# A hybrid attention block on one core: first rows turned by a product with a diagonal, rotary in 1024 columns, queries' sums in the unit stream

## The chip, the core and the metric

The kernel runs on one core of one Trainium2 chip. The core has a matrix engine (TensorE, PE in the profile, with its weight loads shown apart as PEld), three engines that work on 128 partitions (VectorE or DVE, ScalarE or ACT, GpSimd or POOL), a queue engine (SyncE or SP), and DMA queues, which SP, ACT and POOL start. PE writes its products into PSUM, eight banks of 512 fp32 columns. The metric is the device time of one execution in microseconds (us).

## The reference

One decoder layer on x (1024 tokens, 1024 channels), in fp32:

```python
h = rmsnorm(x, norm_w)                       # x * rsqrt(mean(x*x) + eps) * norm_w
proj = h @ w_in                              # 9232 columns
q_a, k_a = rope(q, cos, sin), rope(k, cos, sin)
o_a = dilated_mixture(q_a, k_a, v_a)         # three groups: dilation 1, 4, 16; 8 heads of 64
y_a = (o_a * silu(dsa_z)) @ w_up_a
cqkv = silu(causal_conv(gdn_qkv, conv_w))    # gated delta rule, 8 heads, chunks of 64
gq, gk = l2norm(gq) * 64**-0.5, l2norm(gk)
o_b = rmsnorm(gated_delta_rule(gq, gk, gv, g, beta), gdn_norm_w)
y_b = (o_b * silu(gdn_z)) @ w_up_b
out = rmsnorm(x + (sigmoid(gate_a)*y_a + sigmoid(gate_b)*y_b) @ w_out, final_norm_w)
```

rope takes each head's two halves a, b of 32 channels to a cos - b sin and b cos + a sin. The delta rule needs, per chunk and head, the inverse of a unit lower triangular 64 by 64 matrix.

## The kernel before

**Numbers in two halves.** Every fp32 matrix that enters a large product is split into fp16 high and low parts, and a product is three matmuls (high by high, high by low, low by high). The normalised input, transposed, is kept as h_hi and h_lo (channels on partitions, tokens along the columns) for the whole kernel. ACT makes the high part (a copy to fp16), DVE the low part (a scalar_tensor_tensor, STT, L82, or tensor_tensor, TT, L85; all such operations have the helper's line).

**The start (L390 to L560).** Tokens 0 to 511 come as rows (xt, four blocks of 128 tokens), tokens 512 to 1023 already transposed. For a block of rows, `rstd_rows` (L442) has ACT square and sum, and DVE invert the root; `scale_rows` multiplies the rows by that factor and by the norm weights (nwr, 512 KB, the weights repeated on all partitions); `turn_rows` (L457) has PE transpose eight squares of 128 into two PSUM banks ("G"); `split_rows` (L462) evicts each bank of 512 columns, ACT the high and DVE the low part. Meanwhile `rows_product` (L470) makes the first query and key units, a block of rows at a time. PE's, ACT's and DVE's order is written out by hand there.

**The unit stream.** All other projections are units of 256 weight columns, kept in a list by the class `Feed`. `feed.tick(n)` emits n steps of the current unit; a step, a tick, is three matmuls (12 small ones in V units). A unit has 32 ticks, or 28 where a seven-product scheme (`seven_products`) saves an eighth. `feed.later(n, fn)` emits fn n ticks later, `feed.until(name)` runs to a unit's end, `feed.flush()` until nothing is left for later. PE's order is this program order throughout; the other engines and the queues follow a planner's order, in which `tc.high_priority` moves work ahead.

**Rotary.** A query or key unit gives two channel tiles (a and b) for two halves of 512 tokens. `rope_evict` (L583) copies each from PSUM into a tile rx of 512 columns (three buffers); `rope_half` (L592) makes, when a and b of a half are there, four products with the tables (tabs, 1 MB, cosines and sines), a difference and a sum (ro), and writes each as high (ACT, L607) and low (DVE) parts into pc tiles, in an order by residue modulo the dilation DIL[g] (1, 4, 8 for groups 0, 1, 2), which it reads with a stride. `rope_out` (L611) spreads them by DMAs on SP into Qh, Ql and Ks.

**Attention (`att_run`, L711).** Six sets (group, half of the heads), groups 2, 1, 0, each in 16 steps: scores (PE L767, L769 into bank "S"), masked minimum (DVE L776), exp (ACT L780), transposes (PE L790 into "G"), split (ACT L795, DVE L85 tl), values (PE L813 to L817 into "O"). Between its parts the next set's units run by ticks. For group 0, `combine` (L840) merges the three groups on DVE; its two transposes (PE L876) come TURN_LAG ticks later.

**The linear attention.** After the last set, `decay` makes E by PE, `keys_side` (L1219) sums the keys' squares by `sumsq` (L1189: for two of eight token blocks, four transposes into bank "S", L1196, ACT squares in place, L1201, DVE sums, L1202, then two ticks) and multiplies key pairs (`pairs`, L1205), `solve` (L1253) loads them through DRAM as As, does the triangular solve X of 32 by 32 blocks on DVE, and writes X and its transpose to DRAM (L1275, L1276); they come back as MT and T1p (L1284, L1282, issued on SP). `merge` (L1287) joins the 32 blocks to 64 on PE (L1299, L1314), inside `state_side`. Heads go in two halves, hb 0 and 1. For the queries (L1593 on): after unit ("gdn", hb, 0), Q_LAG[hb] ticks, `pairs`, `spill`, `sumsq`, and for hb 0 STATE_LAG ticks and `state_side(1)`. The sums rq are first used in the scan over chunks that follows gate unit 5. After the scan come output gates, the up projection, the output product and the final norm.

The functions that the change touches:

## Time and profile before

| what | value |
|---|---|
| median of 3 runs | 1096.39 us (1093.91 to 1096.77) |
| the profiled execution, its own time | 1097.13 us |
| its span, first to last instruction | 1095.4 us |
| mean granted TensorE clock | 0.995 |
| busy ACT, POOL | 572.1 us (52%), 65.4 us (6%) |
| DMA moved | 146.89 MB, 134 GB/s |

In a timeline row stand the start and duration in us, engine, line, operation, output and inputs, shapes, and in brackets how long the engine was idle before it and what ended that. In a row of groups stand the count, the busy time in us, the mean of one in ns, and the idle time ahead. In a wait row stand the total, the number and the longest. In a row of stretches stand the length and, for PE, PEld, DVE, ACT and POOL, busy us and instructions, then the granted clock (1 is full), the DMA share and GB/s. Matmuls are pipelined, so PE's durations overlap, and the spacing of starts is what one costs in a row of many.

### The profile page before, as it was taken

How to read it: one execution, taken by the hardware profiler on the slowest of the kernel's cores; microseconds unless marked ns; L12 is line 12 of the kernel's file. 1: busy time of each engine (PE TensorE's matmuls, PEld its weight loads, DVE VectorE, ACT ScalarE, POOL GpSimd, SP SyncE). 2: the span in 40 equal slices, each digit the busy share in tenths (PEclk: the TensorE clock that was granted, in tenths of full speed). 3: DMA queues.
4: the chain of work that ended last, by engine and by line, in shares of the span. 5: the costliest groups of instructions: out<-in, count | busy, mean ns of one | idle time of the engine just before them, and what ended most of it. 6: DMA issues, size and time to landing. Idle time of an engine off the chain costs nothing.

```text
span 1095.4 us, 23858 instructions
## 1 busy us (share of the span) xinstructions
PE 1055.7 (96%) x9426; PEld 641.1 (59%) x9426; DVE 871.8 (80%) x2039; ACT 572.1 (52%) x1296; POOL 65.4 (6%) x115
## 2 busy tenths in 40 slices
PE   6999999999999999989999999998999999999997
PEld 5895585775866855765555554544545554444443
DVE  5798997969879789979975797966478779699944
ACT  6455766667666656547745624234344335343522
POOL 1200000000000000000000000110200000000000
PEclk9999999999999999999999999999999999999999
DMA  8134521622626332641233357766585532763131
GB/s 290 62 94 138 137 64 66 165 81 81 146 67 164 82 115 75 153 111 56 74 121 138 97 137 186 238 214 174 156 280 159 159 113 88 256 224 127 69 131 77
DMA packets 99344, 146.89 MB, mean 134 GB/s; under 512 B 31120, under 2 KB 64400, under 8 KB 98336
## 3 DMA queue, kind: packets, MB, share of 16 engines
q1 hardware_dynamic: 68976, 83.10, 26.4%
q0 software_dynamic: 12320, 44.11, 13.1%
q10 hardware_dynamic: 17936, 18.16, 4.9%
q8 instruction: 74, 1.21, 0.5%
q14 instruction: 38, 0.31, 0.1%
HBM read 89.56 MB, written 36.90 MB: 115 GB/s over the span
## 4 chain that ended last, share of the span: by engine, by line
PE 57%; DVE 29%; ACT 7%; DMA 3%; issue 3%; SPq 1%; ACTq 0%; DVEq 0%
PE ps_mm L181 14%; PE ps_mm L183 13%; PE ps_mm L182 13%; DVE rt L85 3%; DVE wlo L82 3%; DVE ca L82 2%; DVE sm L776 2%; DVE tl L85 2%; DVE ro L85 2%; ACT sm L780 2%; DVE pcAl L85 1%; PE ps_S L183 1%; PE ps_S L182 1%; PE ps_S L181 1%; DVE pcBl L85 1%
## 5 line engine op out<-in xcount | busy, mean ns | idle before, releaser
L183 PE MATMUL ps_mm<-h_hi,wlo 128*128 128x512 f16 (+1 forms) x552 | 208.0, 377 | 0.0
L182 PE MATMUL ps_mm<-h_lo,whi 128*128 128x512 f16 (+1 forms) x492 | 185.3, 377 | 0.8 <-DVE h_lo L85 0.8
L181 PE MATMUL ps_mm<-h_hi,whi 128*128 128x512 f16 (+1 forms) x492 | 185.6, 377 | 0.0
L183 PEld LDWEIGHTS <-wlo 128*128 128x128 f16 x788 | 77.1, 98 | 87.7 <-issue 1.6
L182 PEld LDWEIGHTS <-whi 128*128 128x128 f16 x848 | 83.1, 98 | 71.6 <-issue 4.7
L181 PEld LDWEIGHTS <-whi 128*128 128x128 f16 x848 | 83.2, 98 | 70.6 <-issue 0.3
L181 PE MATMUL ps_mm<-whi,h_hi 128*128 128x256 f16 x384 | 105.7, 275 | 0.0
L182 PE MATMUL ps_mm<-wlo,h_hi 128*128 128x256 f16 x384 | 105.3, 274 | 0.0
L183 PE MATMUL ps_mm<-whi,h_lo 128*128 128x256 f16 x384 | 105.3, 274 | 0.0
L780 ACT ACTIVATE sm<-sm,osb 128x128 f32<-128x128 f32 (+1 forms) x160 | 69.7, 437 | 54.4 <-DVE osb L776 47.7
L85 DVE TENSOR_TENSOR tl<-ps_G,th 128x256 f16<-128x256 f32 (+1 forms) x96 | 51.9, 541 | 19.1 <-ACT th L795 19.0
L85 DVE TENSOR_TENSOR rt<-rx,tabs 128x512 f32<-128x512 f32 x96 | 64.5, 687 | 1.4 <-ACT rx L586 0.4
L776 DVE CUSTOM_DVE_ANT_0 sm<-ps_S,amask 128x128 f32<-128x128 f32 (+1 forms) x192 | 59.4, 347 | 7.0 <-PE ps_S L769 6.9
L82 DVE SCALAR_TENSOR_TENSOR wlo<-wstage,whi 128x1024 f16<-128x1024 f32 x50 | 60.9, 1219 | 3.7 <-ACT whi L164 3.6
L82 DVE SCALAR_TENSOR_TENSOR ca<-xc,cw,ca 128x512 f32<-128x512 f32 x72 | 53.8, 747 | 7.7 <-ACT ca L982 6.9
L790 PE MATMUL ps_G<-cons,sm 128*128 128x128 f32 x280 | 48.7, 276 | 4.5 <-ACT sm L780 3.0
L164 ACT ACTIVATE whi<-wstage 128x1024 f16<-128x1024 f32 x49 | 51.4, 1050 | 2.4 <-ACT gst L921 1.2
L790 PEld LDWEIGHTS ps_G<-cons,sm 128*128 128x128 f32 x280 | 35.6, 141 | 22.1 <-ACT sm L780 7.8
L82 DVE SCALAR_TENSOR_TENSOR whi<-wstage,whi 128x512 f16<-128x512 f32 x60 | 40.5, 687 | 9.3 <-ACT whi L328 8.4
L182 PEld LDWEIGHTS <-h_hi 128*128 128x128 f16 x384 | 45.9, 120 | 1.9
L181 PEld LDWEIGHTS <-h_hi 128*128 128x128 f16 x384 | 45.9, 120 | 1.8
L183 PEld LDWEIGHTS <-h_lo 128*128 128x128 f16 x384 | 45.8, 119 | 1.7
(438 smaller groups left out, 2601.0 us busy)
## 6 DMA issues: line engine op xcount, KB each, us to landing
wstage<-in_w POOLq DMA_DIRECT2D x68, 512.0 KB, 4.7
og<-osb ACTq DMA_DIRECT2D x32, 132.0 KB, 2.3
og<-og SPq DMA_DIRECT2D x32, 132.0 KB, 2.2
gspb<-gst ACTq DMA_DIRECT2D x16, 256.0 KB, 2.5
sga<-gspa SPq DMA_DIRECT2D x8, 512.0 KB, 6.6
wstage<-in_w_up POOLq DMA_DIRECT2D x8, 512.0 KB, 5.6
wos<-in_w_out SPq DMA_DIRECT2D x8, 512.0 KB, 4.1
sgb<-gspb SPq DMA_DIRECT2D x8, 512.0 KB, 5.3
```

What stands on the lines that cost most here:

```text
L82: (eng or V).scalar_tensor_tensor(out, in0, scalar, in1, op0=op0, op1=op1)
L85: (eng or V).tensor_tensor(out, in0, in1, op)
L164: in_turn(SC.activation(hi[:, 4 * c:4 * c + 4], st, AF.Copy, scale=W_SCALE))
L181: PE.matmul(out, lhsT=wh(k), rhs=mh(k), start=first and i == 0, stop=False, skip_group_check=True)
L182: PE.matmul(out, lhsT=wh(k), rhs=ml(k), start=False, stop=False, skip_group_check=True)
L183: last_pe[0] = PE.matmul(out, lhsT=wl(k), rhs=mh(k), start=False, stop=last and i == len(ks) - 1, skip_group_check=True).ins.name
L776: V.tensor_tensor_reduce(P[:, u, :128 * nk], psc[:, u * 256:u * 256 + 128 * nk], mask, -cexp, -NEG, ALU.add, ALU.min, accum_out=osb[:, 256 ...
L780: SC.activation(P[:, u, :128 * nk], P[:, u, :128 * nk], AF.Exp, bias=osb[:, 256 + hd:257 + hd], scale=-1.0, accum_out=osb[:, 260 + hd:261 ...
L790: PE.transpose(pt[:, c:c + 128], P[:, u, i * 128:i * 128 + 128], ident)
```

## The change

Three parts. In the start, `scale_rows` and its weights nwr are gone: `turn_rows` builds a diagonal matrix of the block's factors (DVE) and multiplies the rows by it (fp32 matmuls in place of transposes), and `split_rows` evicts each 128 columns by themselves, with the norm weight of the channel (nw16) as the scale. The rotary works on both channel tiles of a half in one tile of 1024 columns: the residue order is now made by the eviction's write, the tables are stored in that order, one per group, and loaded at a group's first unit into one buffer. The queries' sums of squares are emitted by the stream (`sumsq_steps`), Q_SUMS[hb] ticks apart, into bank "O", and Q_LAG[0] and TURN_LAG grow by four.

```diff
-Q_LAG = (10, 4)
+Q_LAG = (14, 4)
+Q_SUMS = (8, 3)
...
-TURN_LAG = 16
+TURN_LAG = 20
...
         SC.activation(s1, s1, AF.Sqrt, bias=s0, scale=1.0 / D)
         V.reciprocal(s1, s1)
 
-    def scale_rows(t):
-        for c in range(2):
-            x, n = xt[:, t, 512 * c:512 * c + 512], nwr[:, 512 * c:512 * c + 512]
-            STT(x, x, ss[:, 2 * t + 1:2 * t + 2], n, ALU.mult, ALU.mult)
-
     def turn_rows(t):
+
+        V.tensor_scalar(diag[:, t % 2], ident, ss[:, 2 * t + 1:2 * t + 2], None, op0=ALU.mult)
         pts = [bank("G", 2), bank("G", 2)]
         for k in range(KT):
-            PE.transpose(pts[k // 4][:, k % 4 * 128:k % 4 * 128 + 128], xt[:, t, 128 * k:128 * k + 128], ident)
+            PE.matmul(pts[k // 4][:, k % 4 * 128:k % 4 * 128 + 128], lhsT=xt[:, t, 128 * k:128 * k + 128],
+                      rhs=diag[:, t % 2], start=(k % 4 == 0), stop=True, skip_group_check=True)
         return pts
 
     def split_rows(t, pts, cs=(0, 1)):
         for c in cs:
-            p = pts[c].rearrange("p (k n) -> p k n", k=4)
-            hi, lo = [h[:, 4 * c:4 * c + 4, t * 128:t * 128 + 128] for h in (h_hi, h_lo)]
-            SC.activation(hi, p, AF.Copy, scale=H_SCALE)
-            STT(lo, p, H_SCALE, hi, ALU.mult, ALU.subtract)
+            for k in range(4 * c, 4 * c + 4):
+                p = pts[c][:, k % 4 * 128:k % 4 * 128 + 128]
+                hi, lo = [h[:, k, t * 128:t * 128 + 128] for h in (h_hi, h_lo)]
+                SC.activation(hi, p, AF.Copy, scale=nw16[:, k:k + 1])
+                STT(lo, p, nw16[:, k:k + 1], hi, ALU.mult, ALU.subtract)
 
     def rows_product(ps_, w, t, c):
...
     ap = att.enter_context(tc.tile_pool(name="att", bufs=1, side="right"))
     ropex = ctx.enter_context(ExitStack())
     rp = ropex.enter_context(tc.tile_pool(name="rope", bufs=1))
-    tabs = rp.tile([128, 2, S], F32, name="tabs")
-    nc.sync.dma_start(out=tabs, in_=A["tabs"])
+    tabs = {}
+
+    def load_tabs(g):
+
+        if g not in tabs:
+            tabs[g] = rp.tile([128, 2, S], F32, name=f"tabs{g}", tag="tabs", bufs=1)
+            nc.sync.dma_start(out=tabs[g], in_=A["tabs"][g])
+
+    load_tabs(2)
     amask = ap.tile([128, 384], F32, name="amask")
     nc.sync.dma_start(out=amask, in_=A["amask"])
     DIL = (1, 4, 8)
 
-    def rope_evict(p, ct, offset=None, rest=None):
+    def rope_room():
+        return rp.tile([128, 2, 512], F32, name="rx", tag="rx", bufs=2)
+
+    def rope_evict(g, x, p, ct, offset=None, rest=None):
+
+        by = lambda y: y.rearrange("p (n r) -> p n r", r=DIL[g])
+        x = x[:, ct].rearrange("p (r n) -> p n r", r=DIL[g])
         with tc.high_priority(offset=offset):
-            x = rp.tile([128, 512], F32, name="rx", tag="rx", bufs=3)
             if rest is None:
-                SC.copy(x, p)
+                SC.copy(x, by(p))
             else:
-                STT(x, p, -1.0, rest, ALU.mult, ALU.subtract)
-        return x
-
-    def rope_half(g, pt, hf, ab, offset=0):
+                STT(x, by(p), -1.0, by(rest), ALU.mult, ALU.subtract)
+
+    def rope_half(g, pt, hf, x, offset=0):
         d = DIL[g]
         ts = slice(hf * 512, hf * 512 + 512)
         with tc.high_priority(offset=offset):
-            cos, sin = tabs[:, 0, ts], tabs[:, 1, ts]
-            for n, (u, v, op) in (("A", (0, 1, ALU.subtract)), ("B", (1, 0, ALU.add))):
-                t1 = rp.tile([128, 512], F32, name="rt1", tag="rt1", bufs=1)
-                t2 = rp.tile([128, 512], F32, name="rt2", tag="rt2", bufs=1)
-                TT(t1, ab[u], cos, ALU.mult)
-                TT(t2, ab[v], sin, ALU.mult)
-                o = rp.tile([128, 512], F32, name="ro", tag="ro", bufs=2)
-                TT(o, t1, t2, op)
-                ov = o.rearrange("p (n r) -> p r n", r=d)
-                nn = 512 // d
-                dst = [pt[n + x].rearrange("p (r n) -> p r n", r=d)[:, :, hf * nn:hf * nn + nn]
-                       for x in "hl"]
-                SC.copy(dst[0], ov)
-                TT(dst[1], ov, dst[0], ALU.subtract)
+            cos, sin = [tabs[g][:, i:i + 1, ts].to_broadcast([128, 2, 512]) for i in range(2)]
+            t = rp.tile([128, 2, 512], F32, name="rt", tag="rt", bufs=1)
+            TT(t, x, cos, ALU.mult)
+            TT(x, x, sin, ALU.mult)
+            TT(t[:, 0], t[:, 0], x[:, 1], ALU.subtract)
+            TT(t[:, 1], t[:, 1], x[:, 0], ALU.add)
+            nn = 512 // d
+            src = t.rearrange("p a (r n) -> p a r n", r=d)
+            dst = [pt[l].rearrange("p a (r n) -> p a r n", r=d)[:, :, :, hf * nn:hf * nn + nn] for l in "hl"]
+            SC.copy(dst[0], src)
+            TT(dst[1], src, dst[0], ALU.subtract)
 
     def rope_out(pt, pieces):
 
         with tc.high_priority():
             for name, dst, r0, _ in pieces:
                 for hd in range(4):
-                    nc.sync.dma_start(out=dst[r0:r0 + 32, hd], in_=pt[name][32 * hd:32 * hd + 32])
+                    nc.sync.dma_start(out=dst[r0:r0 + 32, hd], in_=pt[name[1]][32 * hd:32 * hd + 32, "AB".index(name[0])])
             for _, dst, r0, twice in pieces:
                 if twice and r0:
                     nc.sync.dma_start(out=dst[64:128], in_=dst[0:64])
 
     def rope_tiles():
-        return {n: rp.tile([128, S], F16, name=f"pc{n}", tag=f"pc{n}", bufs=1) for n in ("Ah", "Al", "Bh", "Bl")}
+        return {n: rp.tile([128, 2, S], F16, name=f"pc{n}", tag=f"pc{n}", bufs=1) for n in "hl"}
 
     def rope_unit(g, tiles, what):
         def start():
+            load_tabs(g)
             pt = rope_tiles()
             pieces = pieces_of(tiles(), what)
-            ab = {}
+            x, n = {}, [0]
 
             def out(c, hf, p, rest=None):
-                ab[c, hf] = rope_evict(p, c, rest=rest)
-                if (1 - c, hf) in ab:
-                    rope_half(g, pt, hf, [ab[0, hf], ab[1, hf]])
-                if len(ab) == 4:
+                first = hf not in x
+                if first:
+                    x[hf] = rope_room()
+                rope_evict(g, x[hf], p, c, rest=rest)
+                if not first:
+                    rope_half(g, pt, hf, x[hf])
+                n[0] += 1
+                if n[0] == 4:
                     rope_out(pt, pieces)
...
 
     def rope_first(g, ws, pieces):
 
-        pts = [rope_tiles(), {}]
-        for n in "AB":
-            both = ap.tile([128, 2, S], F16, name=f"pk{n}", tag="Vh" if n == "A" else "Vl", bufs=2)
-            pts[1][n + "h"], pts[1][n + "l"] = both[:, 0], both[:, 1]
+        pts = [rope_tiles(), {n: ap.tile([128, 2, S], F16, name=f"pk{n}", tag="V" + n, bufs=2) for n in "hl"}]
+
+        def half(pt, banks, hf, *offset):
+            x = rope_room()
+            for ct, p in enumerate(banks):
+                rope_evict(g, x, p, ct, *offset)
+            rope_half(g, pt, hf, x, *offset)
+
         for pt, banks in zip(pts, qk):
-            rope_half(g, pt, 0, [rope_evict(p, ct, 0) for ct, p in enumerate(banks)], 0)
+            half(pt, banks, 0, 0)
         ab = [q, [bank("S", 2), bank("S", 2)]]
         for i, u in ((2, 1), (3, 0), (3, 1)):
...
-            rope_half(g, pt, 1, [rope_evict(p, ct) for ct, p in enumerate(banks)])
+            half(pt, banks, 1)
...
-                        x = rp.tile([128, 4, 128], F32, name="vx", tag="ro", bufs=2)
+                        x = rope_room()[:, 0].rearrange("p (i c) -> p i c", c=128)
...
-    gpool = [rp, "ro", 2]
+    gpool = [rp, "gst", 1]
...
+            room = rp.tile([128, 2, 512], F32, name="hx", tag="rt" if i == 0 else "rx", bufs=1 + i)
-                x[i, j] = rp.tile([128, 512], F32, name="hx", tag=f"rt{j + 1}" if i == 0 else "ro", bufs=1 if i == 0 else 2)
+                x[i, j] = room[:, j]
...
                 V.tensor_reduce(dst[:, t0:t0 + 2], p.rearrange("p (t h c) -> p t h c", t=2, c=64), AX.X, ALU.add)
             feed.tick(2)
+
+    def sumsq_steps(hb, src, dst):
+
+        def step(t0):
+            p = bank("O", 1)
+            for t in (0, 1):
+                for c in range(2):
+                    o = (2 * t + c) * 128
+                    PE.transpose(p[:, o:o + 128],
+                                 src[2 * hb + c][:, 2 * (t0 + t):2 * (t0 + t) + 2].rearrange("p c i -> p (c i)"), ident)
+            with tc.high_priority():
+                SC.activation(p, p, AF.Square)
+                V.tensor_reduce(dst[:, t0:t0 + 2], p.rearrange("p (t h c) -> p t h c", t=2, c=64), AX.X, ALU.add)
+
+        for n in range(4):
+            feed.later(Q_SUMS[hb] * n + 1, lambda n=n: step(2 * n))
 
     def pairs(hb, src, dst):
 
...
         feed.tick(Q_LAG[hb])
         pairs(hb, qT, E[hb])
         spill(hb)
-        sumsq(hb, qT, rq[:, :, 4 * hb:4 * hb + 4])
+        sumsq_steps(hb, qT, rq[:, :, 4 * hb:4 * hb + 4])
         if hb == 0:
             feed.tick(STATE_LAG)
             state_side(1)
     feed.until(("gate", 5))
-    assert not feed.late
+    feed.flush()
     pctx.close()
     fp = ctx.enter_context(tc.tile_pool(name="fin", bufs=1))
     late.append(fp)
...
+    tabs = np.stack([tabs.reshape(128, 2, 2, 512 // d, d).swapaxes(3, 4).reshape(128, 2, S) for d in (1, 4, 8)])
```

More of the change, by code (lines that the diff above doesn't have):

```diff
@@ L100, in hybrid_block @@
     xs = {i: spr.tile([128, KT, 256], F32, name=f"xs{i}") for i in (2, 3)}
-    nwr = spr.tile([128, D], F32, name="nwr")
     def load_xt(t, c):
@@ L112, in hybrid_block @@
         load_xt(0, c)
-    nc.sync.dma_start(out=nwr, in_=A["nwr"])
     cons = base.tile([128, A["cons"].shape[1]], F32, name="cons")
@@ L497, in hybrid_block @@
         rstd_rows(0)
-        scale_rows(0)
         pts = turn_rows(0)
@@ L509, in hybrid_block @@
             rstd_rows(t)
-            scale_rows(t)
         pts = turn_rows(1)
@@ L521, in hybrid_block @@
         rstd_rows(3)
-        scale_rows(3)
         for c in range(2):
@@ L1924, in _layout @@
         "cons": c(cons),
-        "nwr": c(rows(norm_w)),
         "tabs": tabs,
```

## The prediction

> **What bounds the kernel now.** I read the page first (which engine is full), then what TensorE (PE) waited for, then its granted clock in stretches of 10 us, and last the stages that the change touches, in order of time.
>
> ```profile
> PE 1055.7 (96%) x9426; PEld 641.1 (59%) x9426; DVE 871.8 (80%) x2039; ACT 572.1 (52%) x1296; POOL 65.4 (6%) x115
> ```
>
> PE is busy for 96% of a span of 1095.4 us, so 39.7 us is all that can be won without taking work from it. PE's order is written out by hand, so an idle stretch of PE that is removed is won, unless PE then meets a later wait sooner. The waits, by what ended them (total, times, longest):
>
> ```profile
> PE ps_G L460 <- DVE xt L82: 8.7, 2, 8.4
> PE ps_G L790 <- ACT sm L780: 3.0, 5, 0.8
> PE ps_G L876 <- DVE f L82: 2.2, 1, 2.2
> PE ps_O L817 <- DVE tl L85: 2.2, 4, 0.9
> PE ps_S L1196 <- DVE rq L1202: 2.2, 1, 2.2
> PE ps_S L181 <- ACT rx L586: 1.7, 1, 1.7
> PE ps_G L876 <- DVE mx L85: 1.5, 1, 1.5
> PE ps_G L876 <- DVE osb L85: 1.4, 1, 1.4
> PE ps_S L1215 <- ACT qT L993: 1.3, 1, 1.3
> PE ps_S L1196 <- DVE E L85: 1.2, 1, 1.2
> ```
>
> Each group has its place: L460 is the start, L790 and L817 the attention steps, L876 the turning of the combined heads, L1196 and L1215 the queries of the linear attention. Two of these gaps cost more than they last, as the granted clock (the column ahead of the DMA share) shows:
>
> ```profile
> 470.00:480.00 10.00, 7.75 (x74) 6.39 (x73) 9.02 (x31) 2.13 (x6) 0.00 (x0) 0.83 0.59 143
> 740.00:750.00 10.00, 6.67 (x34) 3.38 (x33) 9.39 (x14) 4.44 (x10) 2.18 (x4) 0.96 1.08 270
> 750.00:760.00 10.00, 10.00 (x102) 5.31 (x101) 4.97 (x8) 4.24 (x8) 0.00 (x0) 0.87 0.42 140
> ```
>
> A mean of 0.83 over 10 us is 3.4 us at half clock, so 1.7 us of work lost; 0.96 and 0.87 together are 3.4 us at half, again 1.7 us. Both follow the 2.2 us waits (L876 and L1196). [...]
>
> **The start.** The diagonal replaces two scalings by one small operation, the transposes by fp32 products, and each eviction of 512 columns by four of 128. The rows (time and duration first):
>
> ```profile
> 5.95 0.16 DVE L450 RECIPROCAL ss<-ss 128x1 f32<-128x1 f32 x1 [5.05 <-ACT ss L449]
> 8.36 1.97 PE L460 MATMUL ps_G<-cons,xt 128*128 128x128 f32 x8 [8.36 <-DVE xt L82]
> 14.76 1.29 PE L460 MATMUL ps_G<-cons,xt 128*128 128x128 f32 x8 [0.39 <-DVE xt L82]
> 15.40 0.16 DVE L450 RECIPROCAL ss<-ss 128x1 f32<-128x1 f32 x1
> 17.67 0.61 PE L476 MATMUL ps_mm<-h_lo,whi 128*128 128x128 f16 x8 [0.98 <-DVE h_lo L82]
> 18.56 1.04 PE L460 MATMUL ps_G<-cons,xt 128*128 128x128 f32 x8
> 19.44 0.61 PE L476 MATMUL ps_mm<-h_hi,whi 128*128 128x128 f16 x8
> 32.88 0.65 PE L422 MATMUL ps_G<-diag,cons 128*128 128x256 f32 x2
> 33.37 0.61 PE L476 MATMUL ps_mm<-h_hi,whi 128*128 128x128 f16 x8
> L1052 ACT ACTIVATE ba<-ps_O 128x128 f32<-128x128 f32 x1 | 0.3, 277 | 2.6 <-PE ps_O L1048 2.6
> L85 DVE TENSOR_TENSOR vn<-un,ps_S 128x128 f32<-128x128 f32 x30 | 7.2, 280 | 8.8 <-PE ps_S L1654 8.8
> ```
>
> The first transposes begin at 8.36 although the reciprocal is done at 6.11: they waited for the norm rows' DMA and a scaling. Now they can begin about 6.4, some 2 us sooner. But 8 transposes hold PE for 19.44 - 18.56 = 0.88 us, 0.11 each. An fp32 product runs as two instructions (the x2 of L422), so a block has 16; at 0.11 each that is 1.76 us, and by the 33.37 - 32.88 = 0.49 us of L422's 256 columns it is 8 x 0.49 / 2 = 1.96. I take 0.88 us more for each of four blocks (bounds 0.8 and 1.1). The second block loses the early start: in DVE's written order diag(1) now stands behind the reciprocal of block 2, which ran at 15.40 because ACT's squares feed it; ACT itself gets eight evictions of 0.28 us a block in place of two. So block 1 turns from about 15.3 to 17.0 instead of 14.76 to 16.0, and evictions of 8 x 0.28 = 2.2 us behind it use up the 0.98 us wait at 17.67. PE is at block 2 at 18.6, as before, and from there to 40 us it had no wait: blocks 2 and 3 lengthen it by 2 x 0.88 = 1.8 us. **Start: +1.8** (from -1, if the early start survives, to +3).
>
> [...]
>
> **Rotary.** Per half of a unit DVE had four products, two sums and two subtractions of 512 columns; it gets two products of 1024, two sums of 512 and one subtraction of 1024; ACT's two casts become one.
>
> ```profile
> L85 DVE TENSOR_TENSOR rt<-rx,tabs 128x512 f32<-128x512 f32 x96 | 64.5, 687 | 1.4 <-ACT rx L586 0.4
> L85 DVE TENSOR_TENSOR kd<-qT,eGl 128x1024 f32<-128x1024 f32 x4 | 4.9, 1223 | 2.5 <-DMA kd_d<-kd 2.0 <-ACT qT L1175 0.5
> L85 DVE TENSOR_TENSOR pcAl<-ro,pcAh 128x512 f16<-128x512 f32 x8 | 8.7, 1093 | 0.6 <-ACT pcAh L607 0.5
> L85 DVE TENSOR_TENSOR pcAl<-ro,pcAh 128x512 f16<-128x512 f32 x6 | 4.1, 683 | 0.0
> L607 ACT CAST pcAh<-ro 128x512 f16<-128x512 f32 x8 | 9.2, 1148 | 6.1 <-DVE ro L85 6.1
> L433 ACT CAST h_hi<-xs 128x1024 f16<-128x1024 f32 x4 | 4.2, 1045 | 9.2 <-DVE xs L82 9.2
> L586 ACT COPY rx<-ps_mm 128x512 f32<-128x512 f32 x27 | 15.5, 580 | 7.9 <-PE ps_mm L183 6.0 <-DVE rt L85 1.9
> ```
>
> The third row is of stage 160 to 300 us (strided reads), the fourth of 300 to 440 (group 0, not strided). Products: 4 x 0.687 - 2 x 1.223 = 0.30 us saved in each of 24 halves; subtraction 2 x 1.093 - 1.223 = 0.96 in the 16 strided halves and 0.14 in the other 8: 7 + 15 + 1 = 23 us of DVE. ACT saves 2 x 1.15 - 1.05 = 1.25 us in the 16 strided halves: 20 us. But the stride moves into the evictions' writes. No row shows a strided write: between 0.58 us, as now, and 1.15, as the strided read, each of 24 ACT copies costs 0 to 0.57 us, 0 to 14 us in all. [...]
>
> These engines are not PE, so I price only waits: the 1.7 us of L181 at 50 us goes, since the fourth eviction waited for a third rx buffer and four halves now have room: **-1.7**. Of L790 and L817 (5.2 us together) I take rather over half, as the rest is latency inside one attention step: **-3.0** (0 to -5). Two more tables of 1 MB are loaded on SP at the start of a group's first unit, a load that waits until DVE has done with the last table; a V unit lies between, and the first use is most of a unit later, so I price it at nothing. Were SP late (the DMAs of rotated heads and the combine's loads stand behind it there), DVE would stand at a product with the attention's work behind it. The gate's spill has one staging buffer in place of two; the next fill is a product of four ticks later, so nothing, or at most 1 us.
>
> **Combine.** A tick is three 512-column matmuls of 0.22 us:
>
> ```profile
> 754.95 0.22 PE ps_mm L181
> ```
>
> Four more ticks give 2.6 us, over the longest wait of 2.2. The three L876 waits (5.1) and the half clock (1.7) make 6.8. The head buffers are held those four ticks longer, and ACT's copy and its DMA move with the turning; no one waits for them but the buffers' next use, a whole round of four blocks later. DVE stays full around the waits, so part moves to the next attention step: **-5.5** (0 to -6.8).
>
> **Queries.** The sums leave bank S and their four pairs of ticks; with four ticks more ahead of the pairs the waits of L1215, L1196 go: 1.3 + 1.2 + 2.2 and the half clock of 1.7 make -6.4. But they covered something. The merge of the second half (L1299) needs the solved blocks, back from DRAM:
>
> ```profile
> 672.43 0.69 DVE L85 TENSOR_TENSOR rv<-ps_O,bg 128x512 f32<-128x512 f32 x1
> 673.58 0.51 SPq L1257 DMA_DIRECT2D As<-m_d  x1
> 723.97 0.33 SPq L1275 DMA_DIRECT2D u_d<-X  x1
> 728.77 0.50 SPq L1276 DMA_DIRECT2D t_d<-T  x1
> L1284 SPq DMA_DIRECT2D MT<-u_d x2: 2047/2994/3941, 743.1 to 745.2; - x2
> DMA to landing us min/median/max: 11.0/11.7/12.5
> 757.47 1.20 PE L1299 MATMUL ps_S<-T1p,MT 32*32 32x32 f32 x64
> ```
>
> The last block is issued at 745.2 and lands 11.0 us later, at 756.2; PE comes at 757.47, so it had 1.3 us to spare. PE now comes earlier: four ticks fewer stand ahead of the merge (2.6), three of four transposing steps move behind it (3 x half of 0.88 = 1.3), and 6.4 us of waits are gone: 757.5 - 10.3 = 747.2. The chain does not move with it: As was loaded behind a DMA that waits for rv, which the unit stream times, then DVE's solve and SP's issues follow; that the keys' side starts 2.6 us later in the stream, behind a longer flush, falls into that wait. So PE would stand for 9.0 us, with the whole unit stream behind L1299 in its order, and run at half clock after it (1.7). **Queries: -6.4 + 9.0 + 1.7 = +4.3** (-6.4 to +6). The second half's sums, three ticks apart in one bank, cost 0 to 2 us: transposes, a square on ACT and a reduction on DVE, by rows of their size 0.44 + 0.58 + 0.69 = 1.7, must pass in 1.9: +0.3.
>
> **Sum.** 1.8 - 1.7 - 3.0 - 5.5 + 4.3 + 0.3 = -3.8 us. The profiled execution took 1097.13 (1.73 around its span), 0.74 over the median of 1096.39: 1097.13 - 3.8 - 0.74 = 1092.6. About 0.3%, 3.3 us, can be told from no change.
>
> **Rivals.** (1) The merge does not wait. For: t_d was issued at 728.77, 4.8 us after X, only because SP stood behind another load, and another order of SP would bring the blocks sooner. Against: the reads back were issued until 745.2 and took over 11 us each, behind other DMAs. Then the queries give -6.4 and the sum is -14.5: 1081.9. Chance 0.20.
> (2) Slower: DVE stays the limit of the attention stages, because strided evictions of 1.15 us stand in ACT's queue ahead of the exps, and the waits of L790, L817 and L876 only move. For: DVE is at 9.0 of 10 us and more there. Against: it loses 23 us. Without those 8.5 us the sum is +4.7: 1101.1. It decides when less than 1.4 us of the 8.5 comes back. Chance 0.15.
> (3) The gains and the new wait cancel: half of the 8.5 comes back: -3.8 + 4.2 = +0.4: 1096.8. Chance 0.20.
>
> **How the numbers follow.** The forecast has 0.45; its own range is 1088 to 1096, with 0.35 faster by over 0.3% and 0.10 within. Rival 1 is faster, rival 3 within, rival 2 slower with 0.12 and within with 0.03: faster 0.55, same 0.33, slower 0.12. The range goes from rival 1 to the lower part of rival 2: 1081 to 1100.
>
> **What would show it.** PE's L460 begins near 6.4, has 16 instructions a block, 1.8 us each in blocks 2 and 3, and PE is later by 1.8 at 40 us; no wait of L181 near 50; no waits of L876; no half clock near 474; rx copies show the price of strided writes. A wait of L1299 of 5 to 11 us, and half clock behind it, is the step I lean on most: without it I am wrong towards rival 1; with waits of L790 grown by several us, towards rival 2.

## The result and the profile after

The changed kernel took 1104.51 us (median of 4 runs, 1102.78 to 1106.57) against 1096.24 for the kernel before on the same chip: 1.0086 times as long, interval 1.0065 to 1.0108. I had forecast 1092.6, and 1100 as the upper end. The profiled execution took 1102.78 us, the least of the four, with a span of 1101.0, 5.6 more than before. Of the executions below one was slow: the rotary alone took 2815.03 us once in ten, which its ratio leaves out, and the median of the other nine is 1092.32.

First the page's busy line and the waits of TensorE (total, times, longest), of the changed kernel, to be held against those of before.

```profile
PE 1062.9 (97%) x9458; PEld 652.1 (59%) x9458; DVE 856.2 (78%) x1987; ACT 566.4 (51%) x1296; POOL 66.3 (6%) x115
```

```profile
PE ps_G L456 <- DVE diag L453: 8.9, 3, 6.0
PE ps_G L421 <- DVE diag L86: 2.9, 1, 2.9
PE ps_O L829 <- DVE tl L86: 2.7, 3, 1.4
PE ps_mm L474 <- ACT whi L163: 2.6, 1, 2.6
PE ps_S L781 <- DMA Ql<-Ql: 2.3, 1, 2.3
PE ps_G L1343 <- DVE Y L86: 1.4, 2, 0.9
```

The long waits of the combine (L876 of before) and of the queries (L1215, L1196) are gone. At the second merge PE waits 1.4 us for DVE (L1343), and not for a block from DRAM. New are waits in the start (L456 is the product with the diagonal, L421 the spreading of the factors of tokens 512 to 1023, L474 the first units' products) and one at the first scores (L781). PE is busy for 7.2 us more with only 32 more instructions (x9458 against x9426). By my estimate of 0.88 us a block the products with the diagonal are some 3.5 us of that, and the granted clock, ahead of the last two columns, was lower too: 0.987 in the mean against 0.995. The stretches of the start, and those that ran below full clock before:

```profile
10.00:20.00 10.00, 5.01 (x48) 4.28 (x48) 4.88 (x11) 6.14 (x19) 0.00 (x0) 0.66 0.87 305
20.00:30.00 10.00, 7.45 (x51) 6.93 (x50) 4.13 (x10) 4.12 (x10) 0.58 (x1) 0.67 0.32 126
30.00:40.00 10.00, 10.00 (x136) 9.94 (x135) 4.39 (x11) 6.70 (x18) 1.83 (x3) 0.82 0.13 41
50.00:60.00 10.00, 9.90 (x116) 9.32 (x117) 5.04 (x11) 5.23 (x7) 1.82 (x2) 0.83 0.32 107
120.00:130.00 10.00, 9.08 (x51) 4.77 (x52) 3.52 (x15) 5.41 (x16) 0.00 (x0) 0.83 0.06 19
470.00:480.00 10.00, 10.00 (x103) 9.11 (x101) 10.00 (x24) 6.67 (x17) 0.53 (x1) 1.00 0.56 152
740.00:750.00 10.00, 10.00 (x146) 5.13 (x148) 5.47 (x10) 4.80 (x9) 0.00 (x0) 1.00 0.99 263
750.00:760.00 10.00, 10.00 (x140) 5.46 (x130) 9.24 (x15) 5.08 (x11) 2.17 (x4) 1.00 0.91 250
```

So the half clocks of 470 us and of 740 to 760 us are gone (microsecond by microsecond, the granted clock before was 0.50 from 473 to 476 and from 750 to 752 us), and the start has four stretches at 0.66 to 0.83 where it had 1.00 (0.50 from 14 to 23, 27 to 33 and 51 to 54 us). To measure the start I take one point that both kernels pass, the second spreading of factors, after which PE goes on to the last quarters. Timeline of PE, before and then after:

```profile
39.15 0.65 PE L422 MATMUL ps_G<-diag,cons 128*128 128x256 f32 x2
```

```profile
5.97 3.78 PE L456 MATMUL ps_G<-diag,xt 128*128 128x128 f32 x16 [5.97 <-DVE diag L453]
19.45 3.78 PE L456 MATMUL ps_G<-diag,xt 128*128 128x128 f32 x16 [1.11 <-DVE diag L453]
27.54 3.78 PE L456 MATMUL ps_G<-diag,xt 128*128 128x128 f32 x16 [1.87 <-DVE diag L453]
39.04 2.00 PE L456 MATMUL ps_G<-diag,xt 128*128 128x128 f32 x16
40.88 0.61 PE L474 MATMUL ps_S<-h_hi,whi 128*128 128x128 f16 x8
57.96 0.65 PE L421 MATMUL ps_G<-diag,cons 128*128 128x256 f32 x2
```

This marker (I call it so below) moved from 39.15 to 57.96: the start lost 18.8 us, and the rest of the kernel won back 18.8 - 5.6 = 13.2 between the two profiled executions (by the medians, 8.3 apart, 10.5). My other terms came to -5.6. Where the start lost it, the evictions of block 0 on ACT and DVE show:

```profile
8.08 0.37 ACT L465 ACTIVATE h_hi<-ps_G,nw 128x128 f16<-128x128 f32 x1 [2.68 <-PE ps_G L456]
8.91 0.37 ACT L465 ACTIVATE h_hi<-ps_G,nw 128x128 f16<-128x128 f32 x1 [0.46 <-DVE h_lo L83]
9.70 0.37 ACT L465 ACTIVATE h_hi<-ps_G,nw 128x128 f16<-128x128 f32 x1 [0.42 <-DVE h_lo L83]
10.48 0.63 ACT L465 ACTIVATE h_hi<-ps_G,nw 128x128 f16<-128x128 f32 x2 [0.42 <-DVE h_lo L83]
```

```profile
8.53 0.34 DVE L83 SCALAR_TENSOR_TENSOR h_lo<-ps_G,nw,h_hi 128x128 f16<-128x128 f32 x1
9.31 0.35 DVE L83 SCALAR_TENSOR_TENSOR h_lo<-ps_G,nw,h_hi 128x128 f16<-128x128 f32 x1 [0.43 <-ACT h_hi L465]
```

Read the brackets across the two engines: ACT's piece of 8.91 waited for DVE's of 8.53, DVE's of 9.31 for ACT's of 8.91, and so on. In these rows they are never at work in one bank at the same time, though the pieces are different columns and ACT needs nothing of what DVE writes. A piece takes 0.79 us (9.70 - 8.91), 0.37 of it work. The pair of ACT in the last row runs without a gap (0.63 us): that is the step from the first bank to the second. So in these rows the order is kept per bank of PSUM: a piece waits for what was written down ahead of it in its bank, on the other engine too, and its engine is idle for 0.42 to 0.46 us ahead of it. My sum had no term for it.

### The profile page after: what moved, and what is told of

Its sections match the earlier page's. It is cut to its first block, busy times and chain, and to the rows that moved or that the text cites. A ratio compares the mean times of both kernels' runs of the same rounds, so it can differ in the third digit from the quotient of the medians.

```text
span 1101.0 us, 23823 instructions
## 1 busy us (share of the span) xinstructions
PE 1062.9 (97%) x9458; PEld 652.1 (59%) x9458; DVE 856.2 (78%) x1987; ACT 566.4 (51%) x1296; POOL 66.3 (6%) x115
## 4 chain that ended last, share of the span: by engine, by line
PE 62%; DVE 23%; ACT 6%; DMA 4%; issue 3%; SPq 2%; POOL 0%; ACTq 0%; DVEq 0%
PE ps_mm L180 15%; PE ps_mm L182 15%; PE ps_mm L181 15%; DVE ca L83 3%; DVE wlo L83 2%; DVE sm L788 2%; DVE rt L86 2%; SPq L618 2%; DVE tl L86 2%; PE ps_S L180 1%; PE ps_S L182 1%; PE ps_S L181 1%; PE ps_G L802 1%; PE ps_G L182 1%; PE ps_G L181 1%
## 5 line engine op out<-in xcount | busy, mean ns | idle before, releaser
L802 PE MATMUL ps_G<-cons,sm 128*128 128x128 f32 x280 | 47.5, 275 | 2.3 <-DVE tl L86 0.8
L327 ACT ACTIVATE whi<-wstage 128x512 f16<-128x512 f32 x60 | 37.1, 626 | 18.4 <-DVE wstage L326 13.3
L180 PE MATMUL ps_mm<-h_hi,wlo 128*128 128x512 f16 x120 | 45.6, 380 | 1.0 <-DVE rx L83 1.0
```

The source lines that it names most:

```text
L180: PE.matmul(out, lhsT=wh(k), rhs=mh(k), start=first and i == 0, stop=False, skip_group_check=True)
L327: in_turn(SC.activation(t[:, b, 0], self.part[name], AF.Copy, scale=W_SCALE))
L802: PE.transpose(pt[:, c:c + 128], P[:, u, i * 128:i * 128 + 128], ident)
```

## The experiments

The theory: the evictions in pieces, in the order high, low, high, low, cost the start its 17 us; the fp32 products cost what I forecast. The rival: the products and the half clock behind them cost it.

### The start

**Four and four.** Only the order of the evictions changes:

```diff
         for c in cs:
-            for k in range(4 * c, 4 * c + 4):
-                ...
-                SC.activation(hi, p, AF.Copy, scale=nw16[:, k:k + 1])
-                STT(lo, p, nw16[:, k:k + 1], hi, ALU.mult, ALU.subtract)
+            for lo_too in (False, True):
+                for k in range(4 * c, 4 * c + 4):
+                    ...
+                    if lo_too:
+                        STT(lo, p, nw16[:, k:k + 1], hi, ALU.mult, ALU.subtract)
+                    else:
+                        SC.activation(hi, p, AF.Copy, scale=nw16[:, k:k + 1])
```

> The changed kernel, where only the order of the first rows' evictions differs: of each bank ScalarE writes its four pieces of h_hi first, then VectorE its four of h_lo, instead of one of each in turn. Theory A (one bank is read by the two engines strictly in turn, so that each piece waits 0.42 us for the other engine): the 0.42 us waits go, a block takes 1.5 + 1.5 + 1.4 = 4.4 us in place of 6.3, the product that ends the start (the spread of the second half's factors, at 57.96 us) comes 6 to 10 us sooner, and the time falls from 1104.5 to 1094.5 to 1098.5. Theory B (the fp32 products and the half clock that follows from them make the start long): under 2 us sooner, 1102.5 or more.

Measured: 1088.33 us, 0.9917 of the kernel before (0.9902 to 0.9932), 16.2 under the changed kernel. Its ACT and DVE, and PE's marker:

```profile
8.12 1.14 ACT L469 ACTIVATE h_hi<-ps_G,nw 128x128 f16<-128x128 f32 x4 [2.69 <-PE ps_G L456]
17.02 2.17 ACT L469 ACTIVATE h_hi<-ps_G,nw 128x128 f16<-128x128 f32 x8 [1.63 <-PE ps_G L456]
```

```profile
18.19 2.16 DVE L83 SCALAR_TENSOR_TENSOR h_lo<-ps_G,nw,h_hi 128x128 f16<-128x128 f32 x8 [2.42 <-ACT h_hi L469]
```

```profile
15.82 2.05 PE L456 MATMUL ps_G<-diag,xt 128*128 128x128 f32 x16 [1.41 <-DVE diag L453]
43.07 0.65 PE L421 MATMUL ps_G<-diag,cons 128*128 128x256 f32 x2
```

Eight pieces in a row take 2.17 us, 0.27 each, and DVE's eight follow 1.2 us behind. The marker is at 43.07, 14.9 sooner. The same instructions in another order give back nearly all: theory A, and more than the 6 to 10 us that I expected of it, since I had not counted that the clock stays at 1.00 up to 40 us too. DVE's eight also run while ACT's are under way, in the other bank, so it is not the tiles of h_hi and h_lo that make the engines take turns.

**One bank after the other engine's.** In blocks 1 to 3 the pieces of the two banks alternate:

```diff
-        for c in cs:
-            for k in range(4 * c, 4 * c + 4):
+        for k in [4 * c + j for j in range(4) for c in cs]:
```

> The changed kernel, where the pieces of the two banks alternate in blocks 1 to 3 (h_hi and h_lo of a piece of bank 0, then of one of bank 1, and so on; block 0 keeps one bank at a time). Theory A1 (the turn-taking is per bank: an engine may work in one bank while the other engine is in the other): two pieces pass in the 0.79 us that one took, so a block takes 3.5 us and blocks 1 to 3 save 8 us or more: marker 58.0 - 8 to 12, time 1092 to 1097, later than the order by fours (1088.3) since block 0 stays. Theory A2 (the handing over between ScalarE and VectorE costs its 0.42 us whatever bank they are in): the 0.42 us waits stay, 1102 to 1106.

Measured: 1097.02 us, 1.0008 (0.9984 to 1.0032), marker 54.19. ACT's block 1:

```profile
24.52 0.63 ACT L464 ACTIVATE h_hi<-ps_G,nw 128x128 f16<-128x128 f32 x2 [1.20 <-PE ps_G L456]
25.30 0.63 ACT L464 ACTIVATE h_hi<-ps_G,nw 128x128 f16<-128x128 f32 x2 [0.16 <-DVE h_lo L83]
```

Two pieces pass in the 0.78 us that one took, and the wait is 0.16: the turn-taking is per bank, A1. (Each bank is one tile of the program here, so the runs cannot tell a bank from a tile.) The marker moved by 3.8 us, where A1 had 8 to 12: the granted clock was still 0.70 and 0.67 from 10 to 30 us, and block 1's products took 3.64 us. Where the rest of the time's 7.5 us came from stays open.

**The start undone, and the start alone.** The first is the changed kernel with the start of before; the second is the kernel before with the lines marked + and - exchanged.

```diff
+    nc.sync.dma_start(out=nwr, in_=A["nwr"])
...
-        V.tensor_scalar(diag[:, t % 2], ident, ss[:, 2 * t + 1:2 * t + 2], None, op0=ALU.mult)
...
-            PE.matmul(pts[k // 4][:, k % 4 * 128:k % 4 * 128 + 128], lhsT=xt[:, t, 128 * k:128 * k + 128],
-                      rhs=diag[:, t % 2], start=(k % 4 == 0), stop=True, skip_group_check=True)
+            PE.transpose(pts[k // 4][:, k % 4 * 128:k % 4 * 128 + 128], xt[:, t, 128 * k:128 * k + 128], ident)
...
-                SC.activation(hi, p, AF.Copy, scale=nw16[:, k:k + 1])
+            SC.activation(hi, p, AF.Copy, scale=H_SCALE)
...
         rstd_rows(0)
+        scale_rows(0)
```

> The changed kernel with the start as it was before: norm rows loaded, rows scaled, transposes, evictions of 512 columns; rotary, combine and queries stay changed. Theory A (the start alone loses 18.8 us by its marker, and the rest of the change gains 13.2): marker at 39.2 us, 1096.2 - 13.2 = 1083, within 2 us. Theory C (part of the 13.2 us is only the old start's delay coming back, since transfers that were waited for have had 18.8 us more): 1087 to 1093, with the wait at the second merge (L1299 of before) that I had forecast.

Measured: 1086.58 us, 0.9896 (0.9842 to 0.995), with single runs from 1079.37 to 1092.14, marker 39.10: between A and C. A's 13.2 us came from two single executions. By the medians the rest had won 10.5 us, and with the kernel before at 1096.81 us beside this run, 1096.8 - 10.5 = 1086.3 is what came out. The wait of C is there too, for the solved blocks, at the merge's second level and of 2.5 us:

```profile
PE ps_G L1349 <- DMA MT<-u_d: 2.5, 1, 2.5
```

> The kernel before with the start alone changed: diagonal products, norm weights at eviction. Theory A: marker near 58 us instead of 39.2, and the time 1096.2 + 18.8 = 1115, within 2 us. Theory C (later waits take up part of the delay): 1103 to 1111.

Measured: 1116.07 us, 1.0167 (1.0148 to 1.0186), marker 58.88: 19.3 us slower than the kernel before beside it (1096.81). The start's loss is passed on whole to the end.

**Wide evictions behind the products.** One factor serves 512 columns, so this kernel leaves out the norm weights of the first 512 tokens.

```diff
-            for k in range(4 * c, 4 * c + 4):
-                ...
+            p = pts[c].rearrange("p (k n) -> p k n", k=4)
+            hi, lo = [h[:, 4 * c:4 * c + 4, t * 128:t * 128 + 128] for h in (h_hi, h_lo)]
+            SC.activation(hi, p, AF.Copy, scale=H_SCALE)
+            STT(lo, p, H_SCALE, hi, ALU.mult, ALU.subtract)
```

> The changed kernel, where the first rows' evictions take 512 columns again with the one factor of 16; the norm weights of the first 512 rows are left out, the diagonal products stay. It prices the fp32 products without the evictions in pieces. Theory A: an fp32 block costs 0.9 us more than its transposes, the marker is at 39 to 43 us and the time 1083 to 1088. Theory B (products and half clock): marker beyond 50 us, 1097 or more.

Measured: 1086.79 us, 0.991 (0.9889 to 0.9931), marker

```profile
41.98 0.65 PE L421 MATMUL ps_G<-diag,cons 128*128 128x256 f32 x2
```

So the diagonal's products cost 41.98 - 39.15 = 2.8 us, inside my bounds (-1 to +3), and the granted clock is 1.00 in every stretch up to 60 us. Theory B is out.

**Filled gaps.** How much of the 18.8 us is half clock? PE gets products of the unit matrix, read by nobody, in the longer gaps.

```diff
+        filler(10)
         rows_product(q, wq, 0, 1)
+        filler(8)
...
+        filler(10)
         pts = turn_rows(2)
...
+        filler(14)
         pb = spread(2)
```

> The changed kernel with TensorE kept busy in the start's longer gaps by 10, 8, 10 and 14 products of the unit matrix that nobody reads (2.2, 1.8, 2.2 and 3.1 us at full clock). It parts the start's loss of 18.8 us into its two halves. Theory H (by the rows, 8 us of it is work at half clock that lies on the path, since each eviction waits for its turned block): the clock stays at 1.0 from 20 to 60 us and the marker comes 5 to 9 us sooner, 1095.5 to 1099.5. Theory I (the evictions' turn-taking alone sets the pace and the slow clock lies in its shadow): marker within 2 us of 58.0, 1102 to 1106.

Measured: 1099.29 us, 1.0033 (1.0016 to 1.0049). By its time that is H; by its marker it is I:

```profile
14.63 4.28 PE L482 MATMUL ps_O<-cons 128*128 128x128 f32 x20
21.92 1.95 PE L456 MATMUL ps_G<-diag,xt 128*128 128x128 f32 x16
57.04 0.65 PE L421 MATMUL ps_G<-diag,cons 128*128 128x256 f32 x2
```

The marker is only 0.9 sooner, with the granted clock at 1.00 in every stretch up to 60 us. But the first filler ran at about half speed itself (4.28 us for 20 instructions, against 2.45 for the 20 from 26.96 us on) and pushed block 1's turn from 19.45 to 21.92; from there to the marker it is 35.1 us in place of 38.5. So the half clock costs some 3.4 us on that path, or more by what the fillers themselves hold up, and the turn-taking most of the loss. Between the two profiled executions (1102.78 and 1099.15) the time fell by 3.6 us. Beside the marker's 0.9 that is the first scores: a wait of 1.5 us in place of 2.3, and full clock from 120 to 130 us, worth 1.7. A clean division of the loss stays open.

**The factors of block 2 later.** On top of four and four:

```diff
-        for t in (1, 2):
-            rstd_rows(t)
+        rstd_rows(1)
         pts = turn_rows(1)
         split_rows(1, pts)
+        rstd_rows(2)
```

> The changed kernel with evictions by fours (1088.3), and the factors of block 2 put behind the turning and eviction of block 1, so that block 1's diagonal no longer stands behind block 2's reciprocal. There block 1's first product began at 15.82, 0.3 us behind a reciprocal of 15.42 that it does not need. Expected: it begins near 14.3 and the start's marker comes 1 to 2 us sooner (41 to 42 in place of 43.1): 1086.3 to 1087.3. If ScalarE's squares of block 2, now behind the evictions, come too late for block 2's turn: no gain, 1088 to 1089.

Measured: 1087.76 us, 0.9918 (0.9887 to 0.9948). Block 1's turn began at 14.17 in place of 15.82, but block 2's then waited 1.31 for its own diagonal, and the marker gained 0.7. In time it cannot be told from four and four.

### The other parts

**Rotary alone** (below, against the changed kernel with the old start), and **the same with flat writes**, which leaves out the reordering of the tokens:

```diff
-Q_LAG = (14, 4)
+Q_LAG = (10, 4)
-TURN_LAG = 20
+TURN_LAG = 16
...
-        sumsq_steps(hb, qT, rq[:, :, 4 * hb:4 * hb + 4])
+        sumsq(hb, qT, rq[:, :, 4 * hb:4 * hb + 4])
```

```diff
-        by = lambda y: y.rearrange("p (n r) -> p n r", r=DIL[g])
-        x = x[:, ct].rearrange("p (r n) -> p n r", r=DIL[g])
+        by = lambda y: y
+        x = x[:, ct]
```

> The kernel before with the rotary part alone changed (tables of three groups, products of 1024 columns, strided eviction). By my forecast: the wait at 50 us and part of the attention waits go, -4.7: 1092, with strided evictions of 0.58 to 1.15 us each. Theory D (ScalarE's dearer evictions and the later loading of the first heads take it back: 1.05 us for each copy in the stage of 90 to 300 us, and a new wait of 2.3 us at the first scores): 1095 to 1098.

> The kernel before with the rotary part alone changed, and the evictions written without the stride: the reordering of the tokens is left out, so that the rotated values of two groups are wrong. It prices the strided writes, of 1.05 us each on ScalarE and 1.05 on VectorE against 0.58 and 0.68. Theory J (they take back what VectorE's shorter rotary gives, as ScalarE's copies stand ahead of the exponentials): 3 us or more below the strided form's 1093.3, 1087 to 1090. Rival K (they lie beside TensorE's work): 1092 to 1094.

Measured: 1093.28 us (0.9978, 0.996 to 0.9997) and 1090.77 (0.9958, 0.9938 to 0.9978). The groups of ACT's evictions (busy, mean ns) and one row of DVE's timeline, of the changed kernel and then with flat writes:

```profile
L593 ACT COPY rx<-ps_mm 128x512 f32<-128x512 f32 x27 | 24.6, 919 | 13.4 <-PE ps_mm L182 12.3 <-ACT f L869 0.6 <-ACT osb L889 0.5
```

```profile
196.84 1.07 DVE L83 SCALAR_TENSOR_TENSOR rx<-ps_mm,x 128x512 f32<-128x512 f32 x1
```

```profile
L598 ACT COPY rx<-ps_mm 128x512 f32<-128x512 f32 x27 | 15.5, 579 | 15.0 <-PE ps_mm L183 14.8
```

```profile
195.29 0.68 DVE L82 SCALAR_TENSOR_TENSOR rx<-ps_mm,x 128x512 f32<-128x512 f32 x1
```

The mean of 919 mixes flat evictions of group 0 with strided ones; one strided copy takes 1.04 to 1.11 us (rows between 190 and 290 us), near the upper of my bounds (0.58 and 1.15). In time the stride costs some 2 us (ratios 0.9978 and 0.9958), with intervals that overlap: neither J nor K. The rotary alone is nearer to the forecast 1092 than to theory D. One wait of the combine grew in it (its waits of PE):

```profile
PE ps_G L893 <- DVE osb L85: 3.7, 1, 3.7
```

It was 1.4 before. But the wait of 2.2 for f is gone there, and the combine's waits sum to 5.2 us (3.7 and 1.5) against 5.1.

**Combine alone** and **queries alone**, each against the kernel before:

```diff
-TURN_LAG = 16
+TURN_LAG = 20
```

```diff
-Q_LAG = (10, 4)
+Q_LAG = (14, 4)
+Q_SUMS = (8, 3)
...
-        sumsq(hb, qT, rq[:, :, 4 * hb:4 * hb + 4])
+        sumsq_steps(hb, qT, rq[:, :, 4 * hb:4 * hb + 4])
```

> The kernel before with the combine's lag alone raised from 16 to 20 ticks. By my forecast: the three waits of 5.1 us and the half clock behind the longest go: -5.5, 1091.3 (from 0 to -6.8). Rival: VectorE is full there, the waits move to the next attention step: 1095 or more.

Measured: 1089.71 us, 0.9945 (0.9928 to 0.9961): -6.1 us, the forecast number, with the L876 waits gone. Where the time was won is another matter (below).

> The kernel before with the queries part alone changed (14 ticks ahead of the pairs, the sums in the stream). By my forecast: -6.4 of waits, but 9.0 us of waiting at the start of the second merge and half clock behind it: +4.3, 1101. Theory E (the solved blocks travel with the first merge, and the last of them is needed only at the merge's second level, some 5 us behind its start): a wait of 0 to 3 us at that second level, -6.4 + 3 or less: 1090 to 1094.

Measured: 1095.6 us, 1.0002 (0.9985 to 1.0018). PE's timeline and the stretch behind it:

```profile
742.60 0.24 PE L1316 MATMUL ps_S<-T1p,MT 32*32 32x32 f32 x2
747.61 1.84 PE L1316 MATMUL ps_S<-T1p,MT 32*32 32x32 f32 x62 [4.77 <-DMA T1p<-t_d]
```

```profile
750.00:760.00 10.00, 8.98 (x156) 4.72 (x155) 5.05 (x8) 2.91 (x5) 0.00 (x0) 0.77 0.13 33
```

Here is the wait I had leaned on, at the merge's first level (L1316 is L1299 of before), with half clock behind it. It is 4.8 us and not 9.0, and the half clock behind it (0.89 from 740 to 750 us, then 0.77) costs 3.4, not 1.7. Theory E's place is not the one here, but that of the kernel with the old start above.

**Queries and combine together** (both diffs).

> The kernel before with queries and combine changed together (14 ticks ahead of the pairs, sums in the stream, and the lag of 20). Alone they gave -0.2 and -6.1 us. Theory F (the edits interact: with the lag of 20, SyncE issues the solved blocks' two stores 2.1 us apart instead of 4.8 and without a load of rvt between them, so the queries' wait of 4.8 us at the second merge shrinks to under 2 and the half clock behind it goes): -11 to -14, 1082 to 1085. Rival G (they only add): -6.3, 1089.5.

Measured: 1088.79 us, 0.9938 (0.9914 to 0.9963). The wait at the merge was gone. The reason stands in SP's timeline, here of the combine alone, to be held against the rows of before in the prediction:

```profile
713.21 1.27 SPq L1341 DMA_DIRECT2D rvt<-rv_d  x2
721.66 0.33 SPq L1275 DMA_DIRECT2D u_d<-X  x1
723.77 0.33 SPq L1276 DMA_DIRECT2D t_d<-T  x1
```

The loads of rvt now stand ahead of X, and t_d is issued 2.1 us behind it, not 4.8. That half of F is shown. The time it promised did not come: 0.9 us under the combine alone, inside the scatter. This run had a new wait of 1.8 us at the first scores and half clock after 750 us (0.83). By its time G holds.

**All but the queries**, on top of four and four (the diff of the queries backwards):

> The changed kernel with evictions by fours, but the queries as before (10 ticks, sums beside the pairs). Alone the queries' part gave -0.2 us, behind the lag of 20 another -0.9. If it is worth no more in the whole: 1088 to 1090. If its 6.4 us of waits are won in the whole (no wait at the second merge there): 1092 to 1095.

Measured: 1093.12 us, 0.9986 (0.9964 to 1.0007), with the old wait and its half clock:

```profile
PE ps_S L1211 <- DVE rq L1217: 2.2, 1, 2.2
```

```profile
740.00:750.00 10.00, 7.83 (x34) 3.90 (x32) 7.69 (x13) 4.80 (x10) 1.07 (x2) 0.83 0.76 253
```

So in the whole kernel the queries' part is worth 1093.12 - 1088.33 = 4.8 us (8.5 - 2.3 = 6.2 if each is set against the kernel before beside it), and alone nothing.

**The first keys on ACT's queue**, on the kernel with block 2 later and on the one with the old start:

```diff
-        for pt, pc in zip(pts, pieces):
-            rope_out(pt, pc)
+        for pt, pc, eng in zip(pts, pieces, (nc.sync, nc.scalar)):
+            rope_out(pt, pc, eng)
```

> The kernel with the factors of block 2 put later, and the first keys' 16 copies issued by ScalarE's queue instead of SyncE's. The changed kernel's first scores waited 2.3 us for the last copy of the queries, which SyncE issued as one of 34 in a row at 0.6 us each. If that row of issues is the cause: the wait and the half clock behind it (1.7 us) go, 2 to 4 us less than without. If ScalarE's 16 issues of 0.34 us (5 us of its time) push the weights' casts back: nothing gained, or 1 to 2 us more.

> The changed kernel with the old start (1086.6, single runs from 1079 to 1092), and the first keys' copies on ScalarE's queue. By the same reasoning 1083; and it tells whether the old start or the new one with evictions by fours is the better base: by the markers (39.2 and 43.1) the old start should be 3 to 4 us ahead.

Measured: 1094.69 us (0.9983, 0.9972 to 0.9993) and 1088.4 (0.9927, 0.9908 to 0.9946), so 6.9 more in the first case and 1.8, inside the scatter, in the second. The wait for Ql is in neither profile, but it was not in that of the first one's base either. A dearer one came, from the first of the two, and below it SyncE's and ScalarE's issues of that line (least, median and greatest in ns, first and last start):

```profile
PE ps_G L805 <- ACT sm L795: 7.5, 4, 4.9
```

```profile
L621 SPq DMA_DIRECT2D Qh<-pch x48: 507/589/1362, 71.1 to 450.1; - x48
L621 ACTq DMA_DIRECT2D Ks<-pkh x8: 557/659/2120, 77.9 to 90.2; - x8
L621 ACTq DMA_DIRECT2D Ks<-pkl x8: 514/578/930, 80.5 to 95.0; - x8
```

Issues that I had put at 0.34 us each took 0.51 to 2.12 us, and all 16 held ACT's queue from 77.9 to 95 us; the work behind them, the first exps among it, came late. With this edit the old start is the better base (1088.4 against 1094.69); without it the two starts cannot be told apart (1086.58 and 1087.76).

## Why the prediction was wrong

**The start, +1.8 forecast, +18.8 measured.** This step failed. I wrote "ACT itself gets eight evictions of 0.28 us a block in place of two", "8 x 0.28 = 2.2 us", and "from there to 40 us it had no wait". The 0.28 was right (0.27 in a row of eight), and the products were right in kind: 1.84 us a block at full clock (39.04 to 40.88), first product at 5.97 against 6.4. But I priced ACT's evictions alone and let DVE's run beside them. In the written order each goes through the same bank in turn, so a block takes 8 x 0.79 = 6.3 us and not 2.2. PE's gaps that follow (2.6 us up to 15.60, 1.1 up to 19.45, 1.9 up to 27.54, 2.9 up to 50.02) brought the half clock (0.50 from 14 to 23, 27 to 33 and 51 to 54 us; with fillers in the longer ones the clock read 1.00 up to 60 us), for which I had left no term here: I had shown from the rows that it follows gaps of 2.2 us, and used that only for gaps far behind the start. The last block's evictions, in ACT's queue ahead of the squares of tokens 512 to 1023, gave the 2.9 us of L421.

**The rx wait, -1.7.** Gone at 50 us; a wait for DVE's rx of 0.4 us grew to 1.0.

**Attention, -3.0.** L790 and L817 with all releasers came to 6.1 us before (3.0, 0.9 and 2.2). In the changed kernel L802 (0.8, 0.7 and 0.6) and L829 (2.7) come to 4.8: 1.3 won. And I had no term for the wait of 2.3 us at the first scores, nor for the half clock behind it, 1.7 (0.83 from 120 to 130). The last copy of Ql lands late there. Counted from the marker it is issued 0.9 us later (111.06 - 57.96 = 53.1, against 91.38 - 39.15 = 52.2 before), and its landing took up to 9.7 us, where before no copy of that line up to 130 us took over 6.4 (later ones took up to 10.5). The wait stands in eight of the ten profiles that have the rotary part with SyncE issuing the copies (0.2 us in the rotary alone, 1.2 to 2.4 in the others), but also in one of the five without it (1.8 with queries and combine). What makes it land late stays open.

**Combine, -5.5.** The number came out (-6.1), the mechanism only in part, so there was luck in it. In the profile of the combine alone the L876 waits are gone, but L817 waits 4.7 us in place of 2.2, and the clock is 0.83 from 480 to 490 us: the half clock has moved. PE at the first merge, before and in the combine alone, and at the second merge in the combine alone:

```profile
682.38 1.20 PE L1299 MATMUL ps_S<-T1p,MT 32*32 32x32 f32 x64
```

```profile
679.74 1.20 PE L1299 MATMUL ps_S<-T1p,MT 32*32 32x32 f32 x64
750.96 1.20 PE L1299 MATMUL ps_S<-T1p,MT 32*32 32x32 f32 x64
```

From the marker (39.15 and 39.58) to the first merge it is 3.1 us less, no more than the 3.6 less of the queries alone, whose edit acts only behind the first merge. From there to the second merge it is 71.2 us in place of 75.1: 3.9 less, where I had counted nothing. The waits of L1215 (1.3) and of L1196 for E (1.2) and the half clock after 740 us are not in that profile; why they went stays open.

**Queries, +4.3.** Alone -0.2: the mechanism was right, its size was not. I took the last block (issued 745.2, landed 756.2) for the one that the merge's first product needs, with 1.3 us to spare. It needs T1p first, and a later level the last MT. With the queries alone that T1p was issued at 734.88 and landed 12.7 us later, at 747.6. Before, it was issued at 738.57 and landed 11.9 us later, at 750.5, 7.0 ahead of PE at 757.47. From the first merge to the second PE took 757.47 - 682.4 = 75.1 us before; with the queries alone it stood after 742.8 - 678.7 = 64.1, 11.0 less (I had 10.3). The T1p took 0.8 longer to land: 11.0 - 7.0 + 0.8 = 4.8, as measured. In the whole kernel the wait did not come at all, which is my rival 1; its reason ("another order of SP would bring the blocks sooner") held: t_d is issued 2.1 us behind X there too (737.83 and 735.72). But I had not seen that the edit of the combine makes that order. I had costed the parts as if they could not touch each other's queues.

**Rival 2** named the strided evictions, and their price was near its upper bound; it was not what made the kernel slower. No rival of mine lay in the start.

**The faster version.** With four and four, 1088.33 us; with the old start, 1086.58; both beat both kernels, and which of them is better the runs don't tell. Most of that gain needs one number: the kernel before with the combine's lag of 20 alone took 1089.71 us.

## What to carry to other kernels

When an eviction is cut into pieces, look at who shares the bank: here a piece cost 0.79 us with two engines in turn in one bank, and 0.27 in a row of one engine's pieces. So write all of one engine's pieces and then all of the other's, or give them different banks (two pieces in 0.78 us here), and price the piece by the round through both engines. In or behind some of PE's gaps of 1.1 to 2.9 us the granted clock was 0.50 here, for some 3 to 10 us: a new gap needs a term for that, at the start too. Parts of a change that look independent on the engines may meet in the order of a queue, as here the combine's lag brought t_d 2.1 us behind X in place of 4.8: look for the DMA that each wait hangs on, block by block, before adding them up.

## What the runs showed of the hardware

- A piece of 128 columns takes 0.37 us on ACT by itself and 0.27 in a row of eight. When two engines take turns in a bank, each waits 0.42 to 0.46 us between its pieces, of which the other engine's piece is 0.34 to 0.37.
- The eviction of 512 fp32 columns with a stride in its write takes 1.04 to 1.11 us on ACT instead of 0.58, and 1.07 on DVE instead of 0.68.
- PE's first products with the diagonal ran at about half speed, 3.78 us for 16 instructions against 2.05 in the next block of four and four, though the clock's column says 1.00 for those first 10 us.
- A gap's length alone did not decide on the half clock: behind the wait of 2.2 us at L1196 the stretches after 740 us read 0.96 and 0.87 before, and 1.00 with the combine alone, which has the same wait, but not the one of 1.2 us ahead of it.
- Sixteen DMA issues in a row on ACT's queue took 0.51 to 2.12 us each and held it from 77.9 to 95 us; on SP's queue the median issue of that line was 0.59 us, and single issues of other shapes on ACT's queue took 0.33 to 0.43.
